# A decoder block on one core: gate chunks stored in eight pieces, a denser background, and the last 128 experts multiplied as a dense block

## Chip, core and metric

The kernel runs on one core of a Trainium2 chip. The metric is the device time of one execution in microseconds (us); the median of three runs of the kernel before is 1910.51 us (1909.21 to 1910.72).

## What is computed

One decoder layer over 256 tokens of width 2048 in float32. The first half (adaLN modulation, a mixer of gMLP and mLSTM heads, an output projection) is not touched. The change lies in the second half, the PEER layer: 8 heads each choose 16 of 16384 one-neuron experts by product keys, and an expert's number is `i1 * 128 + i2`.

```python
q = (x @ w_query).reshape(T, 8, 2, 128)
s1 = einsum("thc,kc->thk", q[:, :, 0], sub_keys_1);  s2 = einsum("thc,kc->thk", q[:, :, 1], sub_keys_2)
v1, i1 = top_k(s1, 16);  v2, i2 = top_k(s2, 16)
cand_s = (v1[..., :, None] + v2[..., None, :]).reshape(T, 8, 256)
cand_i = (i1[..., :, None] * 128 + i2[..., None, :]).reshape(T, 8, 256)
top_s, top_pos = top_k(cand_s, 16);  idx = take_along_axis(cand_i, top_pos, -1)
gates = softmax(top_s)
act = gelu(einsum("td,thkd->thk", x, expert_down[idx]))
y   = einsum("thk,thkd->td", gates * act, expert_up[idx])
out = rms_norm(x + gate_f * y)
```

## The kernel before

Everything wide is multiplied in float32r after a split of each weight tile into a rounded part `H` (ScalarE, ACT) and a remainder `L` (VectorE, DVE); a product then takes three matmuls, H by the high half of the activations, H by the low half, L by the high half.

**Down stage.** The down projection is not gathered: all 16384 experts are multiplied with all 256 tokens. The loop over `j` (128 steps) takes 128 experts, those of one `i1`, in a step: SyncE (SP) loads 1 MB (`raw`, three buffers), ACT and DVE split it in two halves of 128x1024 (`H` and `L`, three buffers each), TensorE (PE) makes 48 matmuls of 128x256 into `ps_z`, ACT takes the GELU into `actg`, and after every fourth step ACT issues the store of four steps' results to the DRAM table `agD` (line 1021). A row of `agD` belongs to one expert: 256 activations and 256 gates.

**Background.** Between the steps run the top-k searches, the softmax, the gates, two leftover modulation pieces (`ada_gf`) and the building of an expert list, all as entries of a list `bg` with a cost each; after a step, entries are put in as long as the cost spent stays under `BG_RATE` times the step number. Gates come in four chunks of 64 tokens: eight `gate_unit`s fill a tile `gch` of 128x(128x64) on the chip (4 MB), `gate_store` (line 709) lets ACT issue its store to `agD` as one transfer of 256-byte runs, and `gate_mask` (lines 715 to 719) takes a maximum over tokens on DVE in two parts, so that it is known which experts any token uses. At its end, `list_a` to `list_d` put the used experts into blocks of 128: those used by tokens 0 to 127 alone, those used by both token tiles, and those used by tokens 128 to 255 alone. `open_up` then opens the buffers of the next stage.

**Up stage.** A block `b` is two gathers by GpSimd (POOL): 128 rows of the up table (`uraw`, 1 MB, ring of `NR` = 5) and 128 rows of `agD` (`agr`, 256 KB, ring of `NA` = 4). ACT and DVE split both, and PE adds 12 matmuls of 128x512 into `ps_y` for each token tile that uses the block: 12 or 24. The loop is written out by hand, with counting semaphores and a block count known only at run time; a barrier of all engines stands ahead of it (`tc.tile_critical`, line 1053). Ahead of the barrier: two blocks are split, three pairs of gathers are issued, `ps_y` is zeroed by eight matmuls (line 1043), and SP loads 4 MB for the last normalization (lines 1048 to 1050). A gather from `agD` waits for all stores to it.

**Queues.** ACT, DVE, PE, POOL and SP each run their instructions in the order in which a list scheduler put them, and an engine that waits holds up everything behind it. A DMA issue is such an instruction: ACT issues the stores to `agD`, SP the loads.

Of the kernel before, what the change touches and what calls it, by code (L numbers as in the profile page):

```python
# [19 lines left out]
P = 128  # L20
D = 2048
# [3 lines left out]
NE = 128  # L25
TOPK = 16
# [3 lines left out]
BG_RATE = 2.35  # L30
TCH = 64
NR, NA, NS, NW = 5, 4, 3, 3
PRE = 3
# [7 lines left out]
def block_kernel(ctx: ExitStack, tc: tile.TileContext, I: dict, out: bass.AP):  # L41
# [6 lines left out]

    agD = dr.tile([NE * P + 1, 2 * T], F32, name="agD")
    agV = agD[0 : NE * P, :].rearrange("(i p) c -> p i c", p=P)  # L50
# [514 lines left out]
    flg = ag.tile([1, P + 1], I32, bufs=1, name="flg")  # L565
    ex_cm = tc.tile_pool(name="ex", bufs=1, reuse_waits="tile")
# [141 lines left out]
    def gate_store(ch):  # L708
        nc.scalar.dma_start(agV[:, :, T + ch * TCH : T + (ch + 1) * TCH], gch[ch])

    def gate_mask(ch, part):
        tt = ch * TCH // P
        sl = slice(part * (P // 2), (part + 1) * (P // 2))
        if ch * TCH % P == 0:
            nc.vector.tensor_reduce(mk[tt][:, sl], gch[ch][:, sl, :], axis=AX.X, op=ALU.max)
        else:
            m = ex.tile([P, P // 2], F32, tag="mr", bufs=2, name="mkp")
            nc.vector.tensor_reduce(m, gch[ch][:, sl, :], axis=AX.X, op=ALU.max)
            nc.vector.tensor_tensor(mk[tt][:, sl], mk[tt][:, sl], m, op=ALU.max)

# [140 lines left out]
    def list_d():  # L861
        ps = ls["ps"]
        v, pad, vi, vg = lt("le", 4)
        V.tensor_scalar(vi, ps[:, 0:P], 128.0, -128.0, op0=ALU.mult, op1=ALU.add)
        V.tensor_tensor(v, vi, ps[:, P : 2 * P], op=ALU.add)
        V.tensor_scalar(pad, ps[:, 0:P], 0.0, float(NE * P + P), op0=ALU.is_equal, op1=ALU.mult)
# [29 lines left out]
    nc.gpsimd.dma_start(agD[NE * P : NE * P + 1, :], zrow)  # L896
# [117 lines left out]
    actg = None  # L1014
    for j in range(NE):
        ps = gemm_t(I["down"][j], hF, "ps_z")
        if j % 4 == 0:
            actg = ag.tile([P, 4, T], F32, tag="actg", bufs=2, name="actg")
        nc.scalar.activation(actg[:, j % 4, :], ps[:, :T], AF.Gelu)
        if j % 4 == 3:  # L1020
            nc.scalar.dma_start(agV[:, j - 3 : j + 1, 0:T], actg)
        background(step)
        step += 1
        if bgi == len(bg) and not R:
            print("background done at", j)
            open_up()
    assert R
# [12 lines left out]
    ps_y = [[bank(f"ps_y{tt}{c}") for c in range(4)] for tt in range(2)]  # L1040
    for tt in range(2):
        for c in range(4):
            mm(ps_y[tt][c], R["z"], R["zm"], start=True, stop=True, skip_group_check=True)
# [4 lines left out]
    nc.sync.dma_start(x1n, x1D.rearrange("a p d -> p a d"))  # L1048
    nc.sync.dma_start(gfb, gfD.to_broadcast([P, D]))
    nc.sync.dma_start(fgb, I["fg"].to_broadcast([P, D]))  # L1050
    nc.scalar.activation(junk, epst, AF.Sqrt)

    with tc.tile_critical():  # L1053
        s_raw = [nc.alloc_semaphore(f"s_raw{i}") for i in range(NR)]
        s_ag = [nc.alloc_semaphore(f"s_ag{i}") for i in range(NA)]
        s_h, s_l, s_m, s_wh, s_wl, s_pe = (nc.alloc_semaphore(n) for n in ("s_h", "s_l", "s_m", "s_wh", "s_wl", "s_pe"))
        S0 = 2
# [13 lines left out]
        with nc.Block() as block:  # L1071

            @block.gpsimd
            def _(g):
                def body(b):
                    if b - NR >= S0:
                        g.wait_ge(s_l, 2 * (b - NR - S0 + 1))
                    k = (b - PRE) // NR
                    gather(R["raw"][b % NR], I["up"], idxU, b).then_inc(s_raw[b % NR], 16)
# [6 lines left out]
            def nth(b, ring):  # L1086
                return len([x for x in range(PRE, b + 1) if x % ring == b % ring])

            @block.scalar
            def _(a):  # L1090
                def body(b):
                    if b >= PRE:
                        a.wait_ge(s_raw[b % NR], 16 * nth(b, NR))
# [12 lines left out]
            def _(v):  # L1106
                def body(b):
                    if b >= PRE:
                        v.wait_ge(s_ag[b % NA], 16 * nth(b, NA))
# [12 lines left out]
                blocks(v, S0, body)  # L1122

# [35 lines left out]
        nc.clear_and_free_semaphores([*s_raw, *s_ag, s_h, s_l, s_m, s_wh, s_wl, s_pe])  # L1159
# [121 lines left out]
```

## Time and profile before

| what | us |
|---|---|
| median of the runs | 1910.51 |
| profiled execution, own time | 1909.96 |
| its span, first to last instruction | 1908.1 |
| PE busy, whole span | 1793.1 |
| DVE / ACT / POOL busy | 1428.6 / 871.9 / 260.4 |
| PE busy in 560 to 1425 (down stage with background), 865 us long | 845.7 |
| PE busy in 1425 to 1500 (from the down to the up stage), 75 us long | 47.0 |
| PE busy in 1500 to 1880 (up stage), 380 us long | 380.0 |
| PE busy in 1880 to 1909 (end), 29 us long | 6.4 |

How to read it: one execution was recorded. A busy engine has an instruction in it; the granted clock is the share of TensorE's full clock of 2.4 GHz that was granted (1.00, or 0.50 for 1.2 GHz, in a mean over a stretch anything between). "Landing" is the time from a DMA's issue to its data's arrival. A time of one stage is read from windows of the trace, and an engine's wait from the entry of the instruction that ended it.

### The profile page before, as it was taken

The page shows a single profiled execution, that of the slowest core. Times are in us where ns is not written, and L with a number is a line of the kernel's source. Part 1 is how long each engine was busy: PE and PEld are TensorE (multiplying, and loading weights), DVE is VectorE, ACT ScalarE, POOL GpSimd, SP SyncE. Part 2 cuts the span into 40 slices and gives each one's busy share as a digit, 9 for nine tenths or more (in the row PEclk, how much of TensorE's full clock was granted, in tenths as well). Part 3 has the DMA queues.
Part 4 walks back from the last instruction along what each step waited for, and adds up shares of the span by engine and source line. Part 5 has one row for each costly group of instructions (what it writes and reads, how often), then busy time and mean ns, then how long its engine had stood idle before and what let it go on. Part 6 is the DMA issues. An engine that isn't in the chain of part 4 may idle for free. (4 is left out here: it accounts for less than half of the span.)

```text
span 1908.1 us, 31719 instructions
## 1 busy us (share of the span) xinstructions
PE 1793.1 (94%) x12792; PEld 1624.9 (85%) x12793; DVE 1428.6 (75%) x2205; ACT 871.9 (46%) x1150; POOL 260.4 (14%) x231
## 2 busy tenths in 40 slices
PE   5889999999899998999899999999995899999995
PEld 3336999999899998999799999999995688888884
DVE  6886898988778875877698667777763677777776
ACT  1016554544544554455244553453332555555654
POOL 0000000000000000000000000000001666656660
PEclk8999999999899999999899999999998899999998
DMA  9997887878465558655869679568545899889992
GB/s 379 347 348 278 338 314 299 300 273 314 153 244 176 188 178 231 207 202 172 238 202 336 216 223 324 212 191 272 181 170 198 322 323 324 316 320 337 332 332 96
DMA packets 153341, 496.42 MB, mean 260 GB/s; under 512 B 76024, under 2 KB 92408, under 8 KB 102240
## 3 DMA queue, kind: packets, MB, share of 16 engines
q1 hardware_dynamic: 47416, 326.50, 46.6%
q0 software_dynamic: 22400, 129.92, 18.9%
q10 hardware_dynamic: 83368, 37.83, 7.2%
q8 instruction: 109, 1.79, 0.4%
q14 instruction: 48, 0.39, 0.1%
HBM read 456.44 MB, written 37.76 MB: 259 GB/s over the span
## 5 line engine op out<-in xcount | busy, mean ns | idle before, releaser
L148 ACT ACTIVATE H<-raw 128x1024 fp32r<-128x1024 f32 x388 | 409.8, 1059 | 604.2 <-PE ps_z L158 404.0
L149 DVE TENSOR_TENSOR L<-raw,H 128x1024 fp32r<-128x1024 f32 x388 | 471.5, 1220 | 250.7 <-ACT H L148 249.7
L157 PE MATMUL ps_z<-hT_f,H 128*128 128x256 f32 x2048 | 588.1, 287 | 16.4 <-ACT H L148 16.4
L159 PE MATMUL ps_z<-hT_f,L 128*128 128x256 f32 x2048 | 582.5, 285 | 2.2 <-DVE L L149 2.2
L158 PE MATMUL ps_z<-hT_f,H 128*128 128x256 f32 x2048 | 582.8, 285 | 0.0
L157 PEld LDWEIGHTS ps_z<-hT_f,H 128*128 128x128 f32 x2048 | 396.2, 193 | 19.0 <-ACT H L148 17.2
L159 PEld LDWEIGHTS ps_z<-hT_f,L 128*128 128x128 f32 x2048 | 395.6, 193 | 3.2 <-DVE L L149 3.2
L158 PEld LDWEIGHTS ps_z<-hT_f,H 128*128 128x128 f32 x2048 | 396.4, 194 | 0.0
L1116 DVE TENSOR_TENSOR uL<-uraw,uH 128x1024 fp32r<-128x1024 f32 x194 | 228.5, 1219 | 101.0 <-ACT uH L1099 101.0
L1099 ACT ACTIVATE uH<-uraw 128x1024 fp32r<-128x1024 f32 x194 | 195.0, 1053 | 172.2 <-PE ps_y L1137 154.0
L1137 PE MATMUL ps_y<-uH,uWH 128*128 128x512 f32 x580 | 229.3, 395 | 27.9 <-issue 27.9
L109 DVE SCALAR_TENSOR_TENSOR acc<-araw,sT,acc 128x512 f32<-128x512 f32 (+1 forms) x240 | 243.9, 1017 | 8.8 <-DMA araw<-ada_sf 4.0
L1137 PE MATMUL ps_y<-uH,uWL 128*128 128x512 f32 x580 | 227.0, 391 | 0.0
L1137 PE MATMUL ps_y<-uL,uWH 128*128 128x512 f32 x580 | 226.9, 391 | 0.0
L985 POOL DMA_INDIRECT agr<-agD,idxG x99 | 141.1, 1425 | 129.6 <-DVE uWL L1118 88.6
L1137 PEld LDWEIGHTS ps_y<-uH,uWH 128*128 128x128 f32 x580 | 110.0, 190 | 50.4 <-issue 28.4
L985 POOL DMA_INDIRECT uraw<-up,idxU x99 | 108.3, 1094 | 176.1 <-DVE idxU L869 141.2
L1137 PEld LDWEIGHTS ps_y<-uH,uWL 128*128 128x128 f32 x580 | 109.5, 189 | 22.8
L1137 PEld LDWEIGHTS ps_y<-uL,uWH 128*128 128x128 f32 x580 | 109.7, 189 | 22.0
L205 PE MATMUL ps_v<-w,xhat 128*128 128x512 f32 x192 | 97.5, 663 | 9.8 <-ACT xhat L176 9.8
L205 PEld LDWEIGHTS ps_v<-w,xhat 128*128 128x128 f32 x192 | 39.2, 211 | 58.8 <-issue 48.3
L157 PE MATMUL ps_q<-hT_f,H 128*128 128x256 f32 x256 | 74.4, 295 | 4.2 <-ACT hT_f L545 3.4
(369 smaller groups left out, 2673.9 us busy)
## 6 DMA issues: line engine op xcount, KB each, us to landing
raw<-down SPq DMA_DIRECT2D x128, 1024.0 KB, 5.0
araw<-ada_sm SPq DMA_DIRECT2D x32, 1024.0 KB, 7.5
raw<-w_ct SPq DMA_DIRECT2D x32, 1024.0 KB, 7.2
araw<-ada_sf SPq DMA_DIRECT2D x32, 1024.0 KB, 6.9
araw<-ada_gm SPq DMA_DIRECT2D x16, 1024.0 KB, 7.0
raw<-w_out SPq DMA_DIRECT2D x16, 1024.0 KB, 6.2
raw<-w_q SPq DMA_DIRECT2D x16, 1024.0 KB, 5.0
araw<-ada_gf SPq DMA_DIRECT2D x16, 1024.0 KB, 7.3
```

Of the source, the lines that this page charges most:

```text
L109: nc.vector.scalar_tensor_tensor(acc, w, sc_, acc, op0=ALU.mult, op1=ALU.add)
L148: nc.scalar.activation(H, r, AF.Copy)
L149: last_l[0] = nc.vector.tensor_tensor(L, r, H.bitcast(F32), op=ALU.subtract).ins
L157: mm(o, H[:, ks], hT[:, k, 0, :], start=first, stop=False)
L158: mm(o, H[:, ks], hT[:, k, 1, :], start=False, stop=False)
L159: mm(o, L[:, ks], hT[:, k, 0, :], start=False, stop=last)
L205: mm(bk, h, w[:, off + c * 512 : off + (c + 1) * 512], start=first, stop=last)
L985: return nc.gpsimd.indirect_dma_start(out_, None, tab, bass.IndirectOffsetOnAxis(ap=idx[:, b : b + 1], axis=0))
L1099: a.activation(H[:, c], raw[:, c], AF.Copy).then_inc(s_h, 1)
L1116: v.tensor_tensor(L[:, c], raw[:, c], H[:, c].bitcast(F32), op=ALU.subtract).then_inc(s_l, 1)
L1137: m_ = t.matmul(ps_y[tt][c], x, y[:, cs], start=False, stop=False, skip_group_check=True)
```

## The change

Five things change.

1. A chunk's store and its mask are cut into eight parts (`GP`); `gate_out` issues one part's store (128x16x64, the last one 128x15x64) and takes the mask of that part. The parts are background entries of 9.4/8 each, where there were two entries of 4.5.
2. `BG_RATE` goes from 2.35 to 2.56, so background work is put in earlier and ends earlier; two blocks of the up stage are split in the third and fourth step after it.
3. The 128 experts with `i1` = 127 leave the list and the table: their mask is cleared, their gates are copied to a tile `gl`, the activations of step 127 stay on the chip, their up rows are loaded by SP and split like a down tile, and they are multiplied as one dense block of 24 matmuls into `ps_y`, in place of its zeroing. So the last store to `agD` follows step 126.
4. Up rows of five blocks, not three, are gathered ahead of the barrier.
5. The 4 MB for the end are loaded by SP in the loop, once 12 blocks are done.

```diff
-BG_RATE = 2.35
+BG_RATE = 2.56
+GP = 8
+PRE, PRR = 3, 5
+TL = 12
-    agD = dr.tile([NE * P + 1, 2 * T], F32, name="agD")
+    agD = dr.tile([NS_E * P + 1, 2 * T], F32, name="agD")
...
-    def gate_store(ch):
-        nc.scalar.dma_start(agV[:, :, T + ch * TCH : T + (ch + 1) * TCH], gch[ch])
-    def gate_mask(ch, part):
+    def gate_out(ch, part):
         tt = ch * TCH // P
-        sl = slice(part * (P // 2), (part + 1) * (P // 2))
+        w = P // GP
+        sl = slice(part * w, (part + 1) * w)
+        e_ = min(sl.stop, NS_E)
+        nc.scalar.dma_start(agV[:, sl.start : e_, cs], gch[ch][:, sl.start : e_, :])
         if ch * TCH % P == 0:
+            nc.vector.tensor_reduce(mk[tt][:, sl], g, axis=AX.X, op=ALU.max)
...
+        if part == GP - 1:
+            nc.scalar.activation(
+                gl[:, ch * TCH : (ch + 1) * TCH], gch[ch][:, P - 1 : P, :].rearrange("p a t -> p (a t)"), AF.Copy
+            )
+            if ch * TCH % P:
+                nc.vector.memset(mk[tt][:, P - 1 : P], 0.0)
...
-        bg.append((0, 4.5, lambda: (gate_store(ch), gate_mask(ch, 0))))
-        bg.append((0, 4.5, lambda: gate_mask(ch, 1)))
+        for part in range(GP):
+            bg.append((0, 9.4 / GP, lambda part=part: gate_out(ch, part)))
...
+        elif j == NE - 2:
+            nc.scalar.dma_start(agV[:, j - j % AB : j + 1, 0:T], actg[:, : j % AB + 1, :])
+        if done_at < j and j - done_at in (3, 4):
+            split(j - done_at - 3, nc.scalar, nc.vector)
...
-    for b in range(2):
-        split(b, nc.scalar, nc.vector)
+    nc.scalar.activation(actg[:, (NE - 1) % AB, :], ps[:, :T], AF.Gelu)
+    dH, dL = load_split(I["up"][NE * P - P : NE * P, :])
+    nc.vector.tensor_tensor(da, actg[:, (NE - 1) % AB, :], gl, op=ALU.mult)
+    nc.scalar.activation(dWH, da, AF.Copy)
+    nc.vector.tensor_tensor(dWL, da, dWH.bitcast(F32), op=ALU.subtract)
+            for n, (x, y) in enumerate(((dWH, dH), (dWH, dL), (dWL, dH))):
+                mm(ps_y[tt][c], x[:, ts_], y[c // 2][:, cs], start=(n == 0), stop=(n == 2), skip_group_check=True)
...
-    gather(R["raw"][2], I["up"], idxU, 2)
+    for b in range(2, PRR):
+        gather(R["raw"][b], I["up"], idxU, b)
...
-            mm(ps_y[tt][c], R["z"], R["zm"], start=True, stop=True, skip_group_check=True)
-    nc.sync.dma_start(x1n, x1D.rearrange("a p d -> p a d"))
-    nc.sync.dma_start(gfb, gfD.to_broadcast([P, D]))
-    nc.sync.dma_start(fgb, I["fg"].to_broadcast([P, D]))
...
+            @block.sync
+            def _(e):
+                _, (n,) = load_regs(e, P, 1, "n")
+                with e.If(n > TL):
+                    e.wait_ge(s_pe, TL)
+                e.dma_start(x1n, x1D.rearrange("a p d -> p a d")).then_inc(s_tl, 16)
+                e.dma_start(gfb, gfD.to_broadcast([P, D])).then_inc(s_tl, 16)
+                e.dma_start(fgb, I["fg"].to_broadcast([P, D])).then_inc(s_tl, 16)
```

On ACT, at the last of the four chunks (line 704 writes `gch`, 709 stores it, 148 is an H, 1019 a GELU, 1021 the store of four steps), before:

```order
L704 ACTIVATE gch<-ps_G 128x4x128 x2
L148 ACTIVATE H<-raw 128x1024 x2
L1019 ACTIVATE actg<-ps_z 128x256
L704 ACTIVATE gch<-ps_G 128x4x128
L1021 DMA agD<-actg 128x4x256
L704 ACTIVATE gch<-ps_G 128x4x128
L709 DMA agD<-gch 128x128x64
L148 ACTIVATE H<-raw 128x1024 x3
L1019 ACTIVATE actg<-ps_z 128x256
```

and the second half of the same chunk now (line 720 stores a part, 152 is an H, 1034 a GELU, 1036 the store of four steps, 728 fills `gl`):

```order
L1036 DMA agD<-actg 128x4x256
L152 ACTIVATE H<-raw 128x1024 x2
L1034 ACTIVATE actg<-ps_z 128x256
L720 DMA agD<-gch 128x16x64
L152 ACTIVATE H<-raw 128x1024 x2
L1034 ACTIVATE actg<-ps_z 128x256
L720 DMA agD<-gch 128x16x64
L1034 ACTIVATE actg<-ps_z 128x256
L720 DMA agD<-gch 128x16x64 x2
L720 DMA agD<-gch 128x15x64
L728 ACTIVATE gl<-gch 128x64
L152 ACTIVATE H<-raw 128x1024 x2
```

One store has become eight, spread over five GELUs; of these, three stand in a row behind a GELU, and between that GELU and the one before it there is no H.

On DVE, ahead of the barrier, before (1011 splits an up block, 1037 multiplies activations and gates of a gathered `agr`, 1039 is the remainder of that product):

```order
L870 CAST idxG<-le 128x128
L869 CAST idxU<-le 128x128
L1011 TENSOR_TENSOR uL_15748<-uraw,uH_15745 128x1024 x2
L1011 TENSOR_TENSOR uL_15749<-uraw,uH_15746 128x1024 x2
L1037 TENSOR_TENSOR agr_15741<-agr_15741 128x256
L1037 TENSOR_TENSOR agr_15742<-agr_15742 128x256
L1039 TENSOR_TENSOR uWL_15754<-agr_15741,uWH_15751 128x256
L1039 TENSOR_TENSOR uWL_15755<-agr_15742,uWH_15752 128x256
```

and now (153 is an L of the down stage, 1054 and 1058 belong to the dense block, 1074 multiplies a gathered `agr`):

```order
L1024 TENSOR_TENSOR uL_15167<-uraw,uH_15164 128x1024 x2
L153 TENSOR_TENSOR L<-raw,H 128x1024 x19
L1081 MEMSET tailbuf 128x1
L1054 TENSOR_TENSOR dact<-actg,gl 128x256
L1074 TENSOR_TENSOR agr_15159<-agr_15159 128x256
L1058 TENSOR_TENSOR dWL<-dact,dWH 128x256
L1074 TENSOR_TENSOR agr_15160<-agr_15160 128x256
L1076 TENSOR_TENSOR uWL_15172<-agr_15159,uWH_15169 128x256
```

The splits of the first two blocks have moved into the down stage; the dense block's `dWL` stands behind the first product that needs a gather.

On PE, at the same place now (1065 is the dense block; before, eight zeroing matmuls stood here):

```order
L1065 MATMUL ps_y_15870<-H,dWH 128x512
L1065 MATMUL ps_y_15870<-L,dWH 128x512
L1065 MATMUL ps_y_15871<-H,dWH 128x512
L1065 MATMUL ps_y_15870<-H,dWL 128x512
L1065 MATMUL ps_y_15871<-L,dWH 128x512
L1065 MATMUL ps_y_15871<-H,dWL 128x512
```

Three of the 24 matmuls stand ahead of the first that reads `dWL`.

## Rows read from the trace of the kernel before

**Rows 1.** The page: its first row.

```profile
span 1908.1 us, 31719 instructions
```

**Rows 2.** Waits of PE, whole span: us in total, times, longest.

```profile
PE ps_y L1137 <- issue: 27.9, 1, 27.9
PE ps_z L157 <- ACT H L148: 16.4, 3, 8.7
```

**Rows 3.** Timeline at the first chunk: start, length, engine; idle before in brackets.

```profile
739.49 0.37 ACTq L709 DMA_DIRECT2D agD<-gch  x1
...
750.75 11.71 ACTq L1021 DMA_DIRECT2D agD<-actg  x1
...
763.68 0.58 PE L157 MATMUL ps_z<-hT_f,H 128*128 128x256 f32 x1 [5.81 <-ACT H L148]
```

**Rows 4.** Windows, PE alone: stretch, length, busy (matmuls), granted clock, DMA share, GB/s.

```profile
757.00:771.00 14.00, 7.73 (x40) 0.63 1.03 292
919.00:935.00 16.00, 6.87 (x37) 0.68 0.98 262
1149.00:1160.00 11.00, 8.63 (x47) 0.69 1.00 305
1306.00:1312.00 6.00, 5.18 (x41) 1.00 0.73 184
...
1485.00:1491.00 6.00, 6.00 (x16) 0.53 0.84 307
...
1500.00:1880.00 380.00, 380.00 (x1686) 1.00 0.88 318
```

**Rows 5.** DMA queues in 741:745, then in 750:755 (two): packets, MB, share.

```profile
q10 hardware_dynamic: 3398, 0.87, 104.8%
...
q1 hardware_dynamic: 261, 1.96, 93.7%
q10 hardware_dynamic: 333, 0.09, 7.5%
```

**Rows 6.** ACT timeline, two GELUs one step apart; page, the two splits.

```profile
949.90 0.37 ACT L1019 ACTIVATE actg<-ps_z 128x256 f32<-128x256 f32 x1
...
955.66 0.37 ACT L1019 ACTIVATE actg<-ps_z 128x256 f32<-128x256 f32 x1
...
L148 ACT ACTIVATE H<-raw 128x1024 fp32r<-128x1024 f32 x388 | 409.8, 1059 | 604.2 <-PE ps_z L158 404.0
L149 DVE TENSOR_TENSOR L<-raw,H 128x1024 fp32r<-128x1024 f32 x388 | 471.5, 1220 | 250.7 <-ACT H L148 249.7
```

**Rows 7.** Timelines of PE, ACT, POOL and DVE between the two stages.

```profile
1455.11 1.90 PE L1043 MATMUL ps_y<-zmv,zst 128*128 128x512 bf16 x7
...
1455.72 0.41 ACTq L1021 DMA_DIRECT2D agD<-actg  x1
...
1475.59 0.95 POOL L985 DMA_INDIRECT agr<-agD,idxG  x1 [20.59 <-issue]
...
1478.09 0.94 POOL L985 DMA_INDIRECT agr<-agD,idxG  x1 [0.30 <-issue]
...
1479.00 0.42 DVE L1037 TENSOR_TENSOR agr<-agr 128x256 f32<-128x256 f32 x1 [14.52 <-DMA agr<-agD,idxG]
...
1484.93 0.79 PE L1137 MATMUL ps_y<-uH,uWH 128*128 128x512 f32 x1 [27.92 <-issue]
```

**Rows 8.** Tile actg: landing of its 32 stores; then DMA queues in 1456:1474.

```profile
DMA to landing us min/median/max: 4.4/6.3/18.0
...
q1 hardware_dynamic: 558, 4.19, 55.3%
```

**Rows 9.** The page's groups: gathers from agD, and one third of the up matmuls.

```profile
L985 POOL DMA_INDIRECT agr<-agD,idxG x99 | 141.1, 1425 | 129.6 <-DVE uWL L1118 88.6
L1137 PE MATMUL ps_y<-uH,uWH 128*128 128x512 f32 x580 | 229.3, 395 | 27.9 <-issue 27.9
```

**Rows 10.** Windows, all engines: PE, PEld, DVE, ACT, POOL busy, clock, DMA.

```profile
560.00:640.00 80.00, 79.94 (x661) 78.93 (x661) 70.75 (x207) 35.33 (x45) 0.00 (x0) 1.00 0.51 179
```

More of the change, by code (lines that the diff above doesn't have):

```diff
@@ L25 @@
 NE = 128
+NS_E = NE - 1
 TOPK = 16
@@ L29 @@
 N_NATIVE_O = 0
-BG_RATE = 2.35
+BG_RATE = 2.56
 TCH = 64
+GP = 8
 NR, NA, NS, NW = 5, 4, 3, 3
-PRE = 3
+PRE, PRR = 3, 5
+AB = 4
+TL = 12
 HP = 100
@@ L47, in block_kernel @@
     psp = ctx.enter_context(tc.tile_pool(name="psp", bufs=8, space=PSUM))
-    agD = dr.tile([NE * P + 1, 2 * T], F32, name="agD")
-    agV = agD[0 : NE * P, :].rearrange("(i p) c -> p i c", p=P)
+    agD = dr.tile([NS_E * P + 1, 2 * T], F32, name="agD")
+    agV = agD[0 : NS_E * P, :].rearrange("(i p) c -> p i c", p=P)
     x1D = dr.tile([2, P, D], F32, name="x1D")
@@ L565, in block_kernel @@
     flg = ag.tile([1, P + 1], I32, bufs=1, name="flg")
+    gl = wp.tile([P, T], F32, tag="rstd", name="gl")
     ex_cm = tc.tile_pool(name="ex", bufs=1, reuse_waits="tile")
@@ L895, in block_kernel @@
     nc.gpsimd.memset(zrow, 0.0)
-    nc.gpsimd.dma_start(agD[NE * P : NE * P + 1, :], zrow)
+    nc.gpsimd.dma_start(agD[NS_E * P : NS_E * P + 1, :], zrow)
     bg = []
@@ L1014, in block_kernel @@
     actg = None
+    done_at = NE
     for j in range(NE):
         ps = gemm_t(I["down"][j], hF, "ps_z")
[L1017 to L1021, printed above, removed]
+        if j % AB == 0:
+            actg = ag.tile([P, AB, T], F32, tag="actg", bufs=2, name="actg")
+        if j < NE - 1:
+            nc.scalar.activation(actg[:, j % AB, :], ps[:, :T], AF.Gelu)
+        if j % AB == AB - 1 and j < NE - 1:
+            nc.scalar.dma_start(agV[:, j - AB + 1 : j + 1, 0:T], actg)
+        elif j == NE - 2:
+            nc.scalar.dma_start(agV[:, j - j % AB : j + 1, 0:T], actg[:, : j % AB + 1, :])
         background(step)
@@ L1025, in block_kernel @@
             print("background done at", j)
+            done_at = j
             open_up()
-    assert R
+        if done_at < j and j - done_at in (3, 4):
+            split(j - done_at - 3, nc.scalar, nc.vector)
+    assert R and done_at + 4 < NE
     up = R["up"]
-    for b in range(2):
-        split(b, nc.scalar, nc.vector)
+    nc.scalar.activation(actg[:, (NE - 1) % AB, :], ps[:, :T], AF.Gelu)
+    dH, dL = load_split(I["up"][NE * P - P : NE * P, :])
+    da = up.tile([P, T], F32, name="dact")
+    nc.vector.tensor_tensor(da, actg[:, (NE - 1) % AB, :], gl, op=ALU.mult)
+    dWH = up.tile([P, T], F32R, name="dWH")
+    nc.scalar.activation(dWH, da, AF.Copy)
+    dWL = up.tile([P, T], F32R, name="dWL")
+    nc.vector.tensor_tensor(dWL, da, dWH.bitcast(F32), op=ALU.subtract)
+    ps_y = [[bank(f"ps_y{tt}{c}") for c in range(4)] for tt in range(2)]
+    for tt in range(2):
+        ts_ = slice(tt * P, (tt + 1) * P)
+        for c in range(4):
+            cs = slice(512 * (c % 2), 512 * (c % 2) + 512)
+            for n, (x, y) in enumerate(((dWH, dH), (dWH, dL), (dWL, dH))):
+                mm(ps_y[tt][c], x[:, ts_], y[c // 2][:, cs], start=(n == 0), stop=(n == 2), skip_group_check=True)
     R["raw"] += [wp.tile([P, 2048], F32, tag="raw", bufs=3, name="uraw") for _ in range(3)]
-    gather(R["raw"][2], I["up"], idxU, 2)
+    for b in range(2, PRR):
+        gather(R["raw"][b], I["up"], idxU, b)
     for b in range(PRE):
@@ L1075, in body @@
                 def body(b):
[L1076 to L1079, printed above, removed]
+                    if b >= PRR:
+                        if b - NR >= S0:
+                            g.wait_ge(s_l, 2 * (b - NR - S0 + 1))
+                        gather(R["raw"][b % NR], I["up"], idxU, b).then_inc(s_raw[b % NR], 16)
                     if b - NA >= S0:
@@ L1084, in _, with nth @@
                 blocks(g, PRE, body)
-            def nth(b, ring):
-                return len([x for x in range(PRE, b + 1) if x % ring == b % ring])
+            @block.sync
[6 more added lines that the diff above has]
+                e.dma_start(fgb, I["fg"].to_broadcast([P, D])).then_inc(s_tl, 16)
+            def nth(b, ring, pre):
+                return len([x for x in range(pre, b + 1) if x % ring == b % ring])
             @block.scalar
@@ L1091, in body @@
                 def body(b):
-                    if b >= PRE:
-                        a.wait_ge(s_raw[b % NR], 16 * nth(b, NR))
+                    if b >= PRR:
+                        a.wait_ge(s_raw[b % NR], 16 * nth(b, NR, PRR))
                     if b - NS >= 0:
@@ L1108, in body @@
                     if b >= PRE:
[L1109 removed]
+                        v.wait_ge(s_ag[b % NA], 16 * nth(b, NA, PRE))
                     g = R["ag"][b % NA]
@@ L1122, in _ @@
                 blocks(v, S0, body)
+                v.wait_ge(s_tl, 48)
             @block.tensor
```

16 lines of the change are left out of this document (8 added, 8 removed).

## Prediction

> **What bounds the kernel now.** I read the stage windows first, then PE's waits, then the timelines at its few idle places. Both long stages are bound by PE. A down step takes 5.76 us, the distance of two GELUs [rows 6], and that is 48 matmuls of 0.12 us; the splits it needs, two H of 1.06 and two L of 1.22 us [rows 6], fit twice over. In the up stage PE is busy in all of 380 us, at 380/1686 = 0.225 us a matmul [rows 4], while POOL's gathers wait for DVE to free buffers, 88.6 us in all [rows 9]: the gathers could run ahead, PE cannot. So only PE's idle places are for sale, and the list of its waits has two that count: 16.4 us in three waits for an H, and one of 27.9 us ahead of the up loop [rows 2].
>
> *The gate stores.* The first chunk's store is issued at 739.49 in 0.37 us, but the next store on ACT, at 750.75, takes 11.71 us to issue, and the H behind it comes so late that PE idles 5.81 us [rows 3]. The queue explains it. With nothing beside it the chunk goes out at 3398/4 = 850 packets of 256 bytes a us; while a down load runs (1.96 MB in 5 us, 0.39 MB a us) only 333 go in 5 us [rows 5]. A chunk is 16384 packets, 19 us alone, and ACT's next issue waits until the chunk is nearly out. 11.71 us of block cost 5.81 us of idle PE, so three ready halves cover about 5.9 us. PE then runs at a mean granted clock of 0.63 to 0.69 around the first three stalls, so part of each stretch is at 1.2 GHz [rows 4]. Idle and slow clock together are the stretch less its matmuls at 0.12 us: 14 - 40x0.12 = 9.2, 16 - 37x0.12 = 11.6, 11 - 47x0.12 = 5.4 and 6 - 41x0.12 = 1.1 us [rows 4]. Sum **27.3 us**.
>
> *Between the stages.* PE ends its last step at 1455.11; the first up matmul is at 1484.93 [rows 7], 29.8 us later, and the next 6 us hold 16 matmuls at a clock of 0.53 [rows 4], 6 - 16x0.225 = 2.4 us lost. Sum **32.2 us**. The chain: the last store to `agD`, issued at 1455.72, is the slow one of its kind (18.0 us to land, median 6.3), beside the 4.19 MB of SP's loads for the end [rows 8]. The first gather from `agD` starts 1.9 us after it has landed, at 1475.59, its product on DVE 3.4 us later, and from the third gather at 1478.09 to the first matmul go 6.84 us, barrier included [rows 7].
>
> **The change part by part.** The sum is made against the profiled execution, 1909.96 us with a span of 1908.1 [rows 1]; its time lies 0.55 us under the median, so the sum holds for either.
>
> *Eight stores a chunk.* The same 16384 packets, but a piece is 2048, 2.4 us alone, and in the rows of ACT the pieces spread over five steps of 5.76 us, 29 us, with H's between. Demand in that time is 19.3 us of packets and five loads of 1.05/0.39 = 2.7 us, 33 us: a little more than there is. So pieces will wait for each other, each for some 2.4 to 5 us of ACT. A step leaves ACT 5.76 - 2x1.06 - 0.37 = 3.3 us, and the ready halves 5.9 us once. At three chunks I find at most two pieces in a row without an H between, or three with full cover: 0, with 5 us if a load falls among the three. The last chunk is different. There a piece, a GELU and three pieces follow each other, and the H that normally stands ahead of the GELU comes behind all of them. From that GELU at T: about 0.9 us for the piece before to get out, 2.4 and 2.4 for the next two, 0.6 for the GELU and the copy to `gl`, 1.06 for the H: 7.4 us, where PE has two halves, 5.76 us. Idle 1.6, with the L of 1.22 behind it about 2.4, with one load among the pieces 5; the slow clock adds about 3. I take **6 us** for all four chunks (0 to 14), so 27.3 - 6 = 21.3 are gained. Issues on ACT rise by 28 x 0.37 = 10 us, in its slack. The masks cost DVE the same in shorter instructions, which lets L's through sooner.
>
> The Trainium skill speaks against this part: its page DMA: Bandwidth & Descriptors, section Rules for kernel authors, wants small transfers combined into one large one, and its measured table asks for 1 MiB a DMA; a piece has half that. Its fit of 2.0 us a DMA plus bytes over 436 GB/s (taken for GpSimd's path) would make 28 more transfers 56 us more, my estimate by that page; the sum would be 1871 + 56 = 1927. By the fit a chunk would take 2.0 + 4.19/0.436 = 11.6 us; the trace has 850 packets a us, 19 us, so packets, not the count of transfers, set the time here, and no run shows the 2 us between two pieces.
>
> *Denser background.* At 2.56 in place of 2.35 DVE's background grows by 9%. In the densest stretch DVE is busy 70.75 of 80 us [rows 10], of which the splits take 2x1.22 a step, 34 us; 37 x 1.09 = 40, together 74 of 80. It fits, with small waits: **1 us** (0 to 5). The end of the background moves ahead by about a tenth of its steps, which is what lets the first two blocks be split under PE's down steps.
>
> *One block of experts less in the list.* Whether the loop gets shorter I counted in the reference on its inputs, gates under the smallest normal float32 taken as unused: 12631 used experts now, in 99 blocks with 27, 46 and 26 of the three kinds, 27 + 2x46 + 26 = 145 products of 12 matmuls. The trace has 99 gathers and 580/4 = 145 [rows 9], so the count is right. Without `i1` = 127 it is 12539 experts, 98 blocks, 27, 45 and 26: 143. So the loop loses 24 matmuls and the dense block has 24: the same work. But 24x0.225 = **5.4 us** of it move out of the loop into the wait ahead of it. The limit is near: 98 blocks hold 12544, five more than counted.
>
> *The way into the up loop.* Let t be the end of PE's last step. The last store now follows step 126 and is issued at t - 5.1; with SP's loads gone it should land in 4.4 to 6.3 us [rows 8], so the first gather starts at t + 1.2 to 3.1 and its data are there at t + 4.6 to 6.5. The dense block does not fill this time, as the rows of DVE show: `dWL` is queued behind the product of that first gather, and on PE three matmuls stand ahead of the first that reads `dWL`. So PE does three, waits, and does the other 21 from t + 5.4 to 7.3, in 4.7 us at full clock or about 8.4 at half (six us held 16 [rows 4]): the end is at t + 10.1 to 15.7. The barrier waits for PE too, and from the last arrival to the first matmul it is 6.84 - 3.4 = 3.4 us: t + 13.5 to 19.1. The third gather gives the same: t + 5 to 6.9, plus 6.84, plus 2.7 for the fifth block's 1 MB queued ahead of it. I take t + 16.5 and 1.2 us of slow clock (0 to 2.4): **17.7** against 32.2, and with the 5.4 a gain of 19.9 (16 to 24).
>
> *Loads for the end.* 4.19 MB go beside the gathers after block 12. Five buffers of up rows stand between them and PE: **1 us** (0 to 8.5).
>
> Sum: 1909.96 - 21.3 - 19.9 + 1 + 1 = **1871 us**.
>
> **The rivals.** (a) *Better*: the store lands early, the clock stays up, and no chunk stalls: 6 + 4 + 1 less, 1860. For it: the cover of 5.9 us; against it: three pieces in a row. (b) *99 blocks*: should the smallest gates not count as zero, the count is 12550 and 146 products: 3x12x0.225 = 8.1 more, 1879. (c) *The loads for the end starve the loop.* Sharing with gathers packet by packet of 8 KB, 4.19 MB and as much of gathers take 8.4/0.39 = 21 us, in which the loop needs 21x0.318 = 6.8 MB [rows 4] and gets 4.2: two blocks short, 8 us if the ring covers nothing, 1879. That the DMA engines take turns between queues by the packet is also what the Trainium skill says (DMA: Bandwidth & Descriptors, section Queues, rings and completion order); the 261 and 333 packets agree. (d) *The cut does nothing*, since the same packets keep ACT blocked as long: the 27.3 stay, 1892. (e) *Slower than before*: loads run beside the pieces nearly all the time, so that each takes 5 us or more, 40 us a chunk against 29 + 5.9; with 10 us of idle, 3 of slow clock and two loads a step where `ada_gf` falls in, 15 to 17 us a chunk: 1871 - 6 + 4x16 = 1929. It decides where loads take over half of DMA time; one load a step takes 2.7 of 5.76 us, just under.
>
> **How the numbers follow.** Forecast 0.57 (1862 to 1879), (a) 0.15, (b) 0.10, (c) 0.07, (d) 0.07, (e) 0.04. The likeliest is 1871; 1858 to 1888 leaves out (d), (e) and the ends. 0.2% of 1910 is 3.8 us, about what a measurement of this kernel can tell from no change. Only (e) is slower: faster 0.95, same 0.01, slower 0.04.
>
> **What would show it.** Right: no issue on ACT over 6 us in the first three chunks, PE idle of 2 to 5 us behind the last chunk's pieces; three dense matmuls, a gap, then 21; the first up matmul 13 to 20 us after the last down matmul; 98 gathers from `agD`, 143 products. Wrong: ACT issues adding up to 10 us a chunk; a dense block in one piece; 99 blocks; a PE gap some 50 us into the loop.

## The result, and the profile after

| what | before | after |
|---|---|---|
| median of the runs, us | 1909.86 (4 runs) | 1889.21 (4 runs, 1886.62 to 1891.05) |
| ratio to before, 95% interval | | 0.9899 (0.9887 to 0.9912) |
| profiled execution, own time / span | 1909.96 / 1908.1 | 1886.62 / 1884.8 |

The change makes the kernel 1.0% faster. The forecast was 1871, 38.9 us faster; 20.6 came, and the time lies 1.2 us above the upper end of the range. The profiled execution is the fastest of its four; the sums below are made against it.

Five distances between matmuls tell by stage where the time went. They come from PE's timeline, from the start of one matmul to the start of the next.

| stretch | before | after | difference |
|---|---|---|---|
| start to the first down matmul | 620.9 | 620.3 | -0.6 |
| first to last down matmul | 834.1 | 824.5 | -9.5 |
| last down to first up matmul | 29.9 | 16.7 | -13.3 |
| first to last up matmul | 401.0 | 401.0 | 0.0 |
| last up matmul to the end | 22.2 | 22.3 | +0.1 |

So the way between the stages gave what was forecast, the down stage gave half, and the up stage, forecast to lose half of its slow start (1.2 of 2.4 us) and 24 matmuls (5.4), gave nothing: all of the slow start went, and twelve matmuls came (2.7).

PE's waits, whole span: us in total, times, longest. They answer [rows 2]. The three waits for an H are shorter (7.2 for 16.4), but waits for an L have grown (5.2 us for 2.2 before, of which 3.0 in one piece), and two waits stand on the way into the up stage.

```profile
PE ps_z L161 <- ACT H L152: 7.2, 3, 3.5
PE ps_z L163 <- DVE L L153: 5.2, 4, 3.0
PE ps_y L1065 <- DVE dWL L1058: 4.1, 1, 4.1
...
PE ps_y L1179 <- issue: 2.6, 1, 2.6
```

Windows of PE at the four chunks, and the up stage: stretch, length, busy (matmuls), granted clock, DMA share, GB/s. They answer [rows 4].

```profile
753.00:757.00 4.00, 3.30 (x28) 1.00 0.67 153
897.00:908.00 11.00, 7.84 (x51) 0.84 0.97 236
1102.00:1107.00 5.00, 2.89 (x22) 1.00 1.05 382
1233.00:1250.00 17.00, 10.54 (x64) 0.70 0.73 194
...
1500.00:1860.00 360.00, 360.00 (x1596) 1.00 0.88 322
```

Read as in the prediction, length less matmuls at 0.12 us: 0.6, 4.9, 2.4 and 9.3, in all 17.2 where before had 27.3. (Summed over all matmuls around each chunk it is 18.4 against 28.4; these two are used below. The profiles of two runs below that leave the pieces as they are, the floor of 1e-30 and `dWL` first, give 22.1 and 21.6 by the same sum, so 18.4 is the low end.) The first three chunks lost most of their cost, 26.95 us down to 8.8; the last one, which cost 1.4 before, now costs 9.7.

ACT at the second and third chunk, after. ACTq is an issue; "x2" is two issues together.

```profile
890.53 3.91 ACTq L720 DMA_DIRECT2D agD<-gch  x2
894.48 5.93 ACTq L720 DMA_DIRECT2D agD<-gch  x1
900.54 1.06 ACT L152 ACTIVATE H<-raw 128x1024 fp32r<-128x1024 f32 x1 [8.68 <-issue]
900.67 2.08 ACTq L720 DMA_DIRECT2D agD<-gch  x1
...
1094.84 8.83 ACTq L720 DMA_DIRECT2D agD<-gch  x2
```

In the second chunk three pieces come without an H between; the second and the third block ACT for 3.5 and 5.9 us, and a fourth, behind one H, for 2.1. In the third chunk two in a row do it: the second of them takes 8.4 us alone. The DMA queues in 1097 to 1103 (packets, MB, share of 16 engines) show why: SP loads a down tile and two tiles of `ada_gf` in that time (q1), and the piece (q10) moves at 1238/6 = 206 packets a us, where the uncut store had 850 alone [rows 5].

```profile
q1 hardware_dynamic: 243, 1.83, 80.4%
q10 hardware_dynamic: 1238, 0.32, 23.2%
```

The last chunk on ACT, then DVE, then PE.

```profile
1229.15 8.24 ACTq L720 DMA_DIRECT2D agD<-gch  x3
...
1237.60 1.99 ACT L152 ACTIVATE H<-raw 128x1024 fp32r<-128x1024 f32 x2
...
1235.24 0.16 DVE L767 COPY cnts<-ps_ls 128x6 f32<-128x6 f32 x1 [3.90 <-PE ps_ls L765]
...
1241.19 3.49 DVE L153 TENSOR_TENSOR L<-raw,H 128x1024 fp32r<-128x1024 f32 x3
...
1238.69 0.58 PE L161 MATMUL ps_z<-hT_f,H 128*128 128x256 f32 x1 [3.48 <-ACT H L152]
1242.46 0.58 PE L163 MATMUL ps_z<-hT_f,L 128*128 128x256 f32 x1 [2.98 <-DVE L L153]
```

The three pieces behind the GELU block ACT for 8.24 us and PE idles 3.5. Then it idles 3.0 more: DVE had first waited 3.9 us for the small product of `list_a` (L765), which stands on PE behind the down matmuls, and then ran the whole of `list_a`, 1235.24 to 1241.19, ahead of the L's, whose H's were there from 1238.6 on. The granted clock, 0.70 in the mean of that window, does the rest.

The way into the up stage: the last down matmul, the dense block and the first up matmul on PE; the last store to `agD` on ACT; the first and third gather from it on POOL; the product that waits for the first, and `dWL` behind it, on DVE. They answer [rows 7].

```profile
1444.82 0.28 PE L163 MATMUL ps_z<-hT_f,L 128*128 128x256 f32 x1
1446.48 0.50 PE L1065 MATMUL ps_y<-H,dWH 128*128 128x512 f32 x1 [1.38 <-ACT dWH L1056]
1451.56 0.80 PE L1065 MATMUL ps_y<-H,dWL 128*128 128x512 f32 x1 [4.12 <-DVE dWL L1058]
1461.50 0.49 PE L1179 MATMUL ps_y<-uH,uWH 128*128 128x512 f32 x1 [2.58 <-issue]
...
1440.62 0.37 ACTq L1038 DMA_DIRECT2D agD<-actg  x1
...
1447.28 0.95 POOL L998 DMA_INDIRECT agr<-agD,idxG  x1 [7.38 <-issue]
...
1451.05 0.95 POOL L998 DMA_INDIRECT agr<-agD,idxG  x1 [0.30 <-issue]
...
1450.74 0.43 DVE L1074 TENSOR_TENSOR agr<-agr 128x256 f32<-128x256 f32 x1 [4.76 <-DMA agr<-agD,idxG]
1451.08 0.42 DVE L1058 TENSOR_TENSOR dWL<-dact,dWH 128x256 fp32r<-128x256 f32 x1
```

With t = 1444.82, the store is issued at t - 4.2, the first gather starts at t + 2.5, its product at t + 5.9, the rest of the dense block at t + 6.7, the first up matmul at t + 16.7. The store was forecast at t - 5.1; the others lie inside their forecasts (t + 1.2 to 3.1, 4.6 to 6.5, 5.4 to 7.3, and 13.5 to 19.1 with 16.5 taken). The dense block ends at 1458.9, 1.1 us after the third gather's data (1451.05 and 6.7 us to landing, 1457.8), so of the two it comes last at the barrier.

The page's groups of the up stage, to set beside [rows 9]: 99 gathers, not 98, and 584/4 = 146 half products, not 143.

```profile
L1179 PE MATMUL ps_y<-uH,uWH 128*128 128x512 f32 x584 | 229.5, 393 | 2.6 <-issue 2.6
...
L998 POOL DMA_INDIRECT agr<-agD,idxG x99 | 138.6, 1400 | 131.0 <-DVE uWL L1159 95.0
```

### The profile page after: what moved, and what is told of

Its sections match the earlier page's. It is cut to its first block, busy times and chain, and to the rows that moved or that the text cites. A ratio compares the mean times of both kernels' runs of the same rounds, so it can differ in the third digit from the quotient of the medians.

```text
span 1884.8 us, 31863 instructions
## 1 busy us (share of the span) xinstructions
PE 1796.2 (95%) x12820; PEld 1628.0 (86%) x12820; DVE 1434.8 (76%) x2248; ACT 875.1 (46%) x1157; POOL 257.9 (14%) x231
## 5 line engine op out<-in xcount | busy, mean ns | idle before, releaser
L1179 PEld LDWEIGHTS ps_y<-uH,uWH 128*128 128x128 f32 x584 | 110.0, 188 | 24.8 <-issue 3.0
L1179 PEld LDWEIGHTS ps_y<-uL,uWH 128*128 128x128 f32 x584 | 109.7, 188 | 22.1
```

The source lines that it names most:

```text
L1179: m_ = t.matmul(ps_y[tt][c], x, y[:, cs], start=False, stop=False, skip_group_check=True)
```

## The experiments

What had to be settled: why the chunks still cost 18.4 us, where the 99th block comes from, and what sets the way into the up stage. Times are medians; the kernel before had 1907.5 to 1908.7 beside these runs.

**One store a chunk again**, with the eight masks and all else as changed.

```diff
-        nc.scalar.dma_start(agV[:, sl.start : e_, cs], gch[ch][:, sl.start : e_, :])
+        if part == 0:
+            nc.scalar.dma_start(agV[:, 0:NS_E, cs], gch[ch][:, 0:NS_E, :])
```

> The changed kernel with each chunk stored in one transfer again (issued with the first of its eight mask steps; masks, rate, dense block and loads as changed). Theory (backlog): the DMA engines are full for the 31 to 38 us of a chunk either way and ACT is blocked for 9 to 13 us of it either way; the cut only puts ready halves between the blocks. Then the four chunks cost as before the change, 28.4 us of PE time over 0.12 us a matmul, where the cut has 18.4: 10 us slower than the changed kernel, 1899. Rival (the cut does nothing and the chunks got cheaper through their new places in the schedule): 1889, the same. Rival (what the prediction held: the cut is worth 21): 1910.

1913.74 us, 1.0035 (1.0024 to 1.0046) of before: 24.5 slower than the changed kernel, and slower than before. Nearest is the third number, the prediction's own price of the cut, though the block of the chunks is not what it was before. ACT at the first chunk, and PE's windows at the four:

```profile
721.73 0.37 ACTq L721 DMA_DIRECT2D agD<-gch  x1
729.87 14.84 ACTq L1037 DMA_DIRECT2D agD<-actg  x1
...
736.00:751.00 15.00, 5.82 (x35) 0.66 0.88 208
896.00:912.00 16.00, 6.93 (x44) 0.68 0.88 221
1103.00:1117.00 14.00, 7.71 (x49) 0.76 0.96 251
1243.00:1260.00 17.00, 8.15 (x50) 0.70 0.89 232
```

The chunks cost 10.8, 10.7, 8.1 and 11.0 us by the windows, 41.7 in all over their matmuls, 13 more than before. The block ends 729.87 + 14.84 - 721.73 = 22.98 us after the chunk's issue. Before, it was 750.75 + 11.71 - 739.49 = 22.97 [rows 3], and over all eight chunks of both kernels it is 22.7 to 23.0, but for the last two of before (24.8 and 29.2), where the DMA engines moved 307 and 331 GB/s beside 273 and 263 at the first two. So at six of the eight the block is 22.9 us less the distance to ACT's next store, which is 11.3, 8.1, 16.8 and 22.5 us away before, 8.1, 8.1, 11.3 and 8.1 here. The new schedule puts the chunks where the store of four steps follows sooner; it has the denser background and the masks in eight parts, and no run takes these two apart. In this schedule the cut is worth 41.7 - 18.4 = 23.3 us; the new places of the chunks take 13.3 of it back.

**The pieces issued by POOL.**

```diff
-        nc.scalar.dma_start(agV[:, sl.start : e_, cs], gch[ch][:, sl.start : e_, :])
+        nc.gpsimd.dma_start(agV[:, sl.start : e_, cs], gch[ch][:, sl.start : e_, :])
```

> The changed kernel with the eight pieces issued by POOL, which has nothing to do in the down stage, in place of ACT. Theory (PE is lost only because ACT is blocked in its issues, not because loads come late): ACT has no issue over 3 us left, the 18.4 us at the chunks go down to 0 to 3, and the time is 1871 to 1875. Rival (the full DMA engines starve the down loads themselves): PE waits for H whose raw is late, 10 us or more remain, 1881 or above. Rival (POOL generates 16384 descriptors so slowly, or gets in the way of DVE, that the chunk buffer comes free late and gate units wait for it): above 1889.

1868.50 us, 0.9798 (0.9781 to 0.9814) of before and 20.7 faster than the changed kernel. PE's windows over the first two chunks, and the tile's row on POOL (ns shortest, median, longest):

```profile
722.00:752.00 30.00, 30.00 (x252) 1.00 0.95 302
872.00:904.00 32.00, 32.00 (x269) 1.00 0.95 300
...
L720 POOL DMA_DIRECT2D agD<-gch x32: 1154/1154/1246, 722.2 to 1208.0; - x32
```

The DMA engines are nearly as full as with ACT's pieces (0.95 for 1.00 and 1.02 in the first two chunks), and PE idles not at all. The down loads even take longer to land (median 12.5 us in 722 to 752, where with ACT's pieces it was 7.4 in 721 to 757), and PE does not wait for them: what cost it its time is ACT standing in its issues. The run changes a second thing, the size of the packets (last section), so it does not show this by itself; the run with the last chunk's pieces spread, below, keeps ACT's packets and loses the cost as well. The Trainium skill (DMA: Bandwidth & Descriptors, section Issuing engine by pattern) gives plain stores to the issuing engines with hardware descriptors, as generally faster; here the other path wins, by 20.7 us: POOL is not held in its issues, and nothing waits behind it in this stage.

**POOL's store in the kernel before**, alone, in two halves a chunk.

```diff
-        nc.scalar.dma_start(agV[:, :, T + ch * TCH : T + (ch + 1) * TCH], gch[ch])
+        for h in (slice(0, P // 2), slice(P // 2, P)):
+            nc.gpsimd.dma_start(agV[:, h, T + ch * TCH : T + (ch + 1) * TCH], gch[ch][:, h, :])
```

> The kernel before with one thing changed: each chunk's store issued by POOL, in two halves of 64 experts (one transfer of a whole chunk doesn't fit POOL's ring). Theory (all that the gate stores cost is ACT's blocked issues): the 28.4 us of PE time at the four chunks go, and nothing else: 1907.7 less 28.4 is 1879, and the rest of the change is worth what lies between that and 1868.5, some 11 us. Rival (the rate, the masks and the cut share in the gain): above 1885.

1882.34 us, 0.9864 (0.9847 to 0.988): 26.4 faster than before, 6.9 faster than the whole change. No wait over 1.2 us is left in the down stage. The way into the up stage is as long as before, 29.6 us from the last down matmul at 1424.73. In the changed kernel with POOL's pieces it is 17.1, and these 12.5 us are most of the 13.8 (1882.34 - 1868.50) that the rest of the change is worth beside POOL's stores:

```profile
1454.33 0.78 PE L1138 MATMUL ps_y<-uH,uWH 128*128 128x512 f32 x1 [27.57 <-issue]
```

**The last chunk's pieces twice as far apart.**

```diff
-            bg.append((0, 9.4 / GP, lambda part=part: gate_out(ch, part)))
+            bg.append((0, (9.4 if ch < 3 else 18.8) / GP, lambda part=part: gate_out(ch, part)))
```

> The changed kernel (1889.2) with the last chunk's eight parts at twice the cost in the background's account, so that they are put in over twice as many steps, with an H between any two. Theory (at the last chunk it is the order on ACT, three pieces behind a GELU without an H, that costs 9.7 us of PE, and the same pieces further apart cost 0 to 2): 7 to 9 us faster, 1880 to 1882. Rival (the 9 us for which ACT is blocked come whole wherever the pieces stand): the same, 1889.

1880.93 us, 0.9862 (0.9845 to 0.9878), 8.3 faster than the changed kernel. PE over the whole of the last chunk has 336 matmuls of 0.12 us in 40.3:

```profile
1210.00:1250.00 40.00, 40.00 (x336) 1.00 1.07 299
```

No issue of a piece takes over 0.73 us there, with the DMA engines as full as ever (1.07). So it was the order of the instructions that cost the 9.7 us, and not the bytes. How much is the order on ACT's part this run does not tell: the edit moved `list_a` on DVE as well, where its parts now stand between the L's.

**A floor under the masks**, so that experts whose gates are all under 1e-30 leave the list.

```diff
-        V.tensor_scalar(m0, mk[0], 0.0, None, op0=ALU.is_gt)
+        V.tensor_scalar(m0, mk[0], FLOOR, None, op0=ALU.is_gt)
```

> The changed kernel with the masks compared with 1e-30 in place of 0, so experts whose gates are all under 1e-30 leave the list (their part of the sum is left out; it is under 1e-30 of an activation). Theory (the chip keeps gates under the smallest normal number, so the list held 12550 experts, six over the limit of 12544): counted in the reference, 12434 experts in 98 blocks and 143 half products; 36 matmuls of 0.225 less, 8.1 us faster than the changed kernel, 1881. Rival (the loop is bound by gathers, not by PE): the same, 1889.

1883.89 us, 0.9869 (0.9851 to 0.9887), 5.3 faster than the changed kernel. The page has 98 gathers and 572/4 = 143 half products:

```profile
L1180 PE MATMUL ps_y<-uH,uWH 128*128 128x512 f32 x572 | 225.7, 395 | 2.9 <-issue 2.9
```

The loop takes 394.6 us for 401.0; eight of its first matmuls stood at half clock here, 1.7 us of the 8.1, and the chunks cost some 3.5 more in this execution.

**`dWL` ahead of the first gathered product.**

```diff
-        nc.vector.tensor_tensor(a[:, 0:T], a[:, 0:T], a[:, T:], op=ALU.mult)
+        with tc.issue_after(dwl_ins):
+            nc.vector.tensor_tensor(a[:, 0:T], a[:, 0:T], a[:, T:], op=ALU.mult)
```

> The changed kernel with one order fixed on DVE: the remainder dWL of the dense block ahead of the first product that needs a gather. Theory: the dense block then runs in one piece from 1446.5 to about 1452 or 1453, the last arrival at the barrier is DVE's last remainder at 1453.5, and the first up matmul comes 3 us later, at 1456.5 in place of 1461.5: 5 us faster, 1884. Rival (POOL's third gather and the loop's first instructions set the barrier's end): at most 1 us, 1888.

1890.25 us (1885.97 to 1896.78): no gain. The dense block runs in one piece from 1454.96 to 1460.8, and PE then waits 8.1 us:

```profile
1454.96 0.50 PE L1065 MATMUL ps_y<-H,dWH 128*128 128x512 f32 x1 [1.38 <-ACT dWH L1056]
1468.94 0.79 PE L1180 MATMUL ps_y<-uH,uWH 128*128 128x512 f32 x1 [8.12 <-issue]
...
1464.00:1465.00 1.00, 0.00 (x0) 0.79 0.32 127
1465.00:1466.00 1.00, 0.00 (x0) 0.50 0.01 4
...
1467.60 2.01 ACT L1141 ACTIVATE uH<-uraw 128x1024 fp32r<-128x1024 f32 x2 [6.17 <-issue]
```

The first up matmul comes 15.6 us after the last down matmul (1453.30), 1.0 less than 16.7. The windows (column six is the DMA share) show the gathers' data ending by 1465.0, and the loop opens on ACT 2.6 us later, while the dense block had ended at 1460.8. So the rival holds: with the dense block out of the way the gathers set the barrier's end, and in the changed kernel they had landed only 1.1 us ahead of that block's end. Behind PE's longer idle time 13 up matmuls ran at half clock, 2.7 us, more than what was won.

**The loads for the end ahead of the barrier again** (on the kernel with POOL's stores; the three loads of SP moved out of the loop).

```diff
-    nc.vector.memset(big[:, 0:1], 0.0)
+    nc.sync.dma_start(x1n, x1D.rearrange("a p d -> p a d"))
+    nc.sync.dma_start(gfb, gfD.to_broadcast([P, D]))
+    nc.sync.dma_start(fgb, I["fg"].to_broadcast([P, D]))
```

> The kernel of e2_pool_store (1868.5) with the 4.19 MB for the end loaded ahead of the barrier again, as before the change. Theory (the way into the loop is set by the bytes between the last store to agD and the gathers behind it; the loads for the end were most of them): the store issued 4 us ahead of PE's last step is nearly through when the loads start, but the three small gathers and the fifth block's 1 MB, 1.8 MB, share the engines with 4.19 MB; at 0.39 MB a us that is up to 10.7 us more between PE's last down matmul and the first up matmul, 17.1 going to 24 to 28, and the time to 1875 to 1880. Rival (the earlier last store and the dense block brought the gain, the loads' place nothing): 17.1 stays, 1868.5.

1877.89 us, 9.4 slower than that kernel. The first gathered product, and so `dWL`, come later: the first matmul that reads `dWL` starts at 1442.55, which with t = 1431.95 is t + 10.6 in place of t + 6.7, and the first up matmul at t + 21.0 in place of t + 17.1:

```profile
1442.55 0.80 PE L1065 MATMUL ps_y<-H,dWL 128*128 128x512 f32 x1 [7.96 <-DVE dWL L1058]
1452.98 0.78 PE L1171 MATMUL ps_y<-uH,uWH 128*128 128x512 f32 x1 [3.65 <-issue]
...
1006.17 0.69 DVE L685 TENSOR_TENSOR oh<-iota,it 128x1024 bf16<-128x1024 bf16 x1 [5.01 <-DMA gfD<-gr__10557]
```

3.9 us, and 1.6 of slow clock behind it: 5.5, under the 7 to 11 expected. The other part of this execution's difference stands elsewhere: 5.4 us around 1006, where DVE waits 5 us for a 2 KB store of `gate_f` to land (1.1 in the kernel with POOL's stores). That wait was not touched, and is in the profile of `dWL` first as well; how often it comes can't be told from one profile a kernel. The four times lie in two pairs, 1874.9 and 1875.7 us, and 1880.1 and 1881.5, with the profiled one in the upper pair; the lower is 6.4 to 7.2 above 1868.5.

**Four up rows, not five, ahead of the barrier** (on the same kernel).

```diff
-PRE, PRR = 3, 5
+PRE, PRR = 3, 4
```

> The kernel of e2_pool_store (1868.5) with up rows of four blocks, not five, gathered ahead of the barrier. Theory (the barrier opens some 3 us after the last gathered byte has landed; PE's wait for dWL lay beside that): the fifth block's 1 MB, 2.7 us at 0.39 MB a us, leaves the way, unless the dense block, which ends 2 to 3 us ahead of the first up matmul, takes its place: 0.5 to 2.7 us faster, 1866 to 1868. Rival (the dense block's end sets it): the same to 0.3 us.

1869.81 us (1866.66 to 1871.48) for 1868.50: no gain.

```profile
1434.45 0.80 PE L1065 MATMUL ps_y<-H,dWL 128*128 128x512 f32 x1 [4.04 <-DVE dWL L1058]
...
1440.59 0.40 PE L1065 MATMUL ps_y<-H,dWL 128*128 128x512 f32 x1
1443.57 0.49 PE L1179 MATMUL ps_y<-uH,uWH 128*128 128x512 f32 x1 [2.58 <-issue]
...
1442.19 2.01 ACT L1140 ACTIVATE uH<-uraw 128x1024 fp32r<-128x1024 f32 x2 [6.13 <-issue]
```

The last gather has landed at 1436.5, which is t + 8.7 (t = 1427.78) where five rows have t + 12.8, but the barrier does not open for it: the dense block, behind `dWL`, goes on to 1441.0, and the loop opens on ACT 1.2 us after that. So the rival holds, and the dense block's end sets the way in. That the way is 1.3 us shorter (15.8) comes from the clock: the part behind `dWL` starts at t + 6.7 as with five rows, and 7 of its matmuls ran at half clock, not 14. Then eight up matmuls at half clock, 1.6 us, take it back.

**Four edits together**: POOL's pieces, a floor at 1.2e-38 (gates under it leave the list), `dWL` first, four up rows; the edits are those shown above, with this floor.

```diff
+FLOOR = 1.2e-38
```

> Four edits on the changed kernel: pieces issued by POOL, masks compared with 1.2e-38 (just over the smallest normal number; gates under it leave the list), dWL ahead of the first gather's product, four up rows ahead of the barrier. Theory on the blocks (only gates under the smallest normal number made the 99th block): the reference counts 12539 experts, 98 blocks, 143 half products, 1716 matmuls in the loop, 8.1 us less. Rival (the chip's gates differ from the reference's by more than that, and e3 got its 98 blocks from other small gates): 99 blocks, 1752 matmuls. Theory on the way in (two chains end within 1 us of each other, the dense block behind dWL and the gathers with the fifth block's 1 MB, so that each edit alone gave 1.0 and 1.3 us): both together 2.5 to 3.5, the first up matmul 13.5 to 14.5 us behind the last down matmul in place of 17.1. Sum from 1868.5: 1857. If each was hidden by something third: 1860.

1859.95 us, 0.9747 (0.9731 to 0.9763) of before: 29.3 faster than the changed kernel. The list has 98 blocks and 143 half products: only gates under 1.2e-38 made the 99th. The way in is 1441.02 - 1428.98 = 12.0 us, 5.1 less than with POOL's pieces alone, where `dWL` first alone gave 1.0 and four rows alone moved no instruction on the chain that came last. Either edit alone leaves the other chain in place, the gathers or the dense block; with both the dense block ends at 1436.5 and the last gather has landed at 1437.6. A slow start of the loop (2.1 us) gives part of it back.

```profile
1441.02 0.79 PE L1181 MATMUL ps_y<-uH,uWH 128*128 128x512 f32 x1 [4.51 <-issue]
...
L1181 PE MATMUL ps_y<-uH,uWH 128*128 128x512 f32 x572 | 225.9, 395 | 4.5 <-issue 4.5
```

**A floor of 1e-12** in the same kernel.

```diff
-FLOOR = 1.2e-38
+FLOOR = 1.0e-12
```

> The kernel of e9_together with 1e-12 in place of 1.2e-38 in the masks: experts whose gates are all under 1e-12 leave the list, so their part of the sum is left out (at most 127 x 1e-12 of an activation a token, where float32 rounds at 6e-8). The reference counts 8632 experts, 68 blocks, 25 + 2 x 19 + 24 = 87 half products in place of 143. Theory (the loop stays bound by PE): 56 x 2.73 = 153 us faster than e9_together, 1704. Rival (the gathers become the bound: 68 blocks of 1.31 MB at 0.39 MB a us are 228 us, 87 halves on PE 237 us, nearly level, and a run of one-tile blocks, 2.73 us of PE each, wants 0.48 MB a us): PE waits for uraw in the loop, 10 to 30 us of it, 1714 to 1735.

1712.60 us, 0.898 (0.8963 to 0.8998) of before. The list has 68 blocks and 348/4 = 87 half products, as counted. The loop stays bound by PE but for one wait of 3.9 us around 1508, with 13 matmuls at half clock behind it, and a slow start. At that wait ACT and DVE stand waiting for gathered data, with the DMA engines full (1.02 in 1490 to 1500, 1.01 in 1500 to 1512): the rival's bound, reached once. 147 us of the 153 came, between the theory and its rival.

## Why the prediction was wrong, step by step

Against the profiled executions (a fall of 23.3 us where 39.0 was forecast; the terms sum to 39.2, which 1871 rounds):

| step | forecast | measured |
|---|---|---|
| gate stores | -21.3 | -10.0 |
| rest of the down stage (density) | +1 | +0.4 |
| between the stages, with slow clock | -14.5 | -15.6 |
| matmuls in the loop | -5.4 | +2.4 |
| loads for the end in the loop | +1 | 0 |
| start and end | 0 | -0.5 |

**Gate stores, the step that failed most.** The bound was read rightly: demand of 33 us against 29, so pieces wait for each other. What failed is the step from there to "at most two pieces in a row without an H between, or three with full cover: 0". It priced a piece at 2.4 to 5 us, as if a backlog were a load's length; the trace has pieces of 5.9 and 8.4. In the second chunk the last pieces come when the DMA engines have long been full (1.02 in 872 to 904), and in the third two loads of `ada_gf` fall beside the down load, which the prediction had only in rival (e). That gives 8.8 us at three chunks in place of 0. The last chunk was named as the different one, with 7.4 us from its GELU to the end of the H behind the pieces (9.5 measured) and a sum near 5.5, and cost 9.7: the L's did not follow the H's by 1.22 us, since `list_a` stood between them on DVE. The prediction looked at ACT's order there and not at DVE's. With the pieces spread this chunk costs nothing; with POOL issuing, none does. The upper bound of 14 for all four was too low by 4.4.

The prediction also took the 27.3 us of before as the cost of an uncut store. It is not a property of the store: with the chunks where the new schedule puts them, one store costs 41.7, so the cut is worth more (23.3) than was forecast for it (21.3), and the schedule costs 13 us that no term held. The rows had half of it: the first chunk's issue, the next store's issue and its length [rows 3] give 22.97; the distance to the next store in the new schedule was not worked out.

The Trainium skill's rule against many small transfers (DMA: Bandwidth & Descriptors, section Rules for kernel authors) was weighed at 56 us more. Applied to this store, whose pieces have 0.5 MB, it points the wrong way: the kernel with 32 transfers is 24.5 us faster than with four, since ACT has work behind each issue. Its turn-taking between queues by the packet (section Queues, rings and completion order) agrees with the piece that fell from 850 to 206 packets a us beside three loads.

**Blocks: rival (b), given a chance of 0.10.** The working was right, the choice wrong: gates under the smallest normal number count on the chip, the list has 12550 experts by the reference, six over 98 blocks, and the loop has 146 half products. The agreement with the trace of before (99 and 145) was taken as proof of the count, but 12631 and 12642, without and with those gates by the reference, both give 99 blocks and 145 halves: it tested nothing. The loop took 401.0 us where 393.2 was forecast (401.0 of before less 2.4 of slow start and 5.4).

**Between the stages: right**, 16.7 for 17.7, with no slow clock in the loop, and each time on the chain within its range (the store, which had none, was 0.9 us late). That `dWL` waits behind a gather was right too, but it cost 1.0 us, since the third gather's chain, which the prediction also worked out, ends almost as late. One reading there was off: by [rows 4] 21 matmuls at half clock are 7.9 us, not 8.4, which takes 0.5 off the upper bounds and changes nothing else. The gain divides so: 5.5 us from the loads for the end, as the run with them ahead shows (with POOL's stores); the other 10 from the rest, of which the earlier last store is the likely part, not tried alone.

**Loads for the end, density:** the first cost nothing (no gap in the loop's 401 us), the second 0.4 us outside the chunks.

**The range** reached to 1888, which would just have held the chunks at their bound of 14 and the 146 products together (1871 + 8 + 8.1 = 1887). The chunks went 4.4 over that bound, and the median lies 2.6 above the profiled execution; the terms that came out lower, some 3 us, did not make up for it. Of the signs named for being right, the gap in the dense block, the 21 matmuls behind it and the 13 to 20 us came; the issue of 8.4 us in the third chunk, issues of 14.6 us in all in the second, the 99 gathers and the 146 products spoke against it.

## What to carry to other kernels

In these runs an issue on ACT's queue blocked ACT until the earlier transfer of that queue was nearly out. Where that shows, measure from issue to the end of the block (here 22.9 us, more where loads were denser), subtract the distance to the next issue, and redo that for the new schedule, since moving either end moves the cost. Before cutting a store up so that its engine can breathe, look for an engine with an empty queue: one word here did what eight pieces did not. A count that agrees with the trace proves only what would have come out otherwise; near a limit, try the doubtful cases against it first. Where two chains end together, as the dense block and the gathers do here, an edit to one of them shows little by itself.

## What the runs showed of the hardware that was not expected

- POOL issued the eight pieces of a chunk, up to 2048 runs each, in a row at 1.15 us each (1.25 at most) and was never held up, where ACT was blocked for up to 8.4 us by the same pieces. The records show the transfers of POOL's queue in 720 to 760 as 1152 packets for 4.16 MB, 3.6 KB a packet, where ACT's queue has 256 bytes a packet:

```profile
q0 software_dynamic: 1152, 4.16, 39.5%
```

- Gates under 1.2e-38 are kept: the comparison with 0 counts them, 99 blocks, and the one with 1.2e-38 does not, 98.
- A 2 KB store took 12.4 us to land beside other traffic in one profile, and DVE waited 5 us for it. What made it late there and not in other profiles stays open.
- What the barrier costs depends on what comes last. The loop opened on ACT 1.2 us after the end of the dense block in the changed kernel (1458.9 to 1460.13), with POOL's pieces (1441.4 to 1442.60) and with four rows (1441.0 to 1442.19). Where the gathers came last it opened 1.9 to 2.0 us after the last one had landed: 1481.7 to 1483.58 before, 1465.6 to 1467.60 with `dWL` first, 1437.6 to 1439.63 with the four edits.
